# A hybrid mLSTM and S5 decoder step: TensorE's order in the S5 part written by hand, S5 tables on all 128 partitions

## The chip, the cores and the metric

The kernel runs on one core of one Trainium2 chip. The metric is device time in microseconds (us) of one execution, as the median of several runs. The engines are named as the profile names them: PE is TensorE (PEld its weight loads), DVE is VectorE, ACT is ScalarE, POOL is GpSimd, and SP is SyncE, whose queue issues nearly all DMAs.

## What is computed

One layer of a decoder trunk, for a prompt of 1,024 tokens and a sample batch of 8 sequences with 4 tokens each, in fp32. Cut to what matters here:

```python
a = rmsnorm(h, ln_mix)                      # [1056 tokens, 1024]
proj = a @ w_in
x_m, z_m, o_m, i_pre, f_pre, x_s, z_s = jnp.split(proj, SPLIT_IDX, axis=-1)   # 512 columns each, gates 4 + 4

# S5: 32 groups of 16 channels, each with 64 complex states
a_re, a_im = mag * cos(li * dt), mag * sin(li * dt)
bu = einsum('blgc,gpc->blgp', u, g * B)                 # complex
xs = associative_scan(x_t = a * x_{t-1} + bu_t)         # complex, along the tokens
y  = Re(einsum('blgp,gcp->blgc', xs, C)) + d_skip * u
yB = gelu(y);  yB = yB * sigmoid(yB @ w_glu + b_glu) * silu(z_s)

hA = mlstm_chunkwise(conv, gates, x_m, z_m, o_m)        # four heads
h  = h + concat([hA, yB]) @ w_out
h  = h + sigmoid(h @ w_ple_gate) * rmsnorm(p @ w_ple)
y  = rmsnorm(h, ln_final)
```

The final states of the mLSTM, the convolution and the S5 part are outputs too.

## The kernel before

**Products.** Large products are made in fp32 precision from two parts of each operand. `wtile` (L94) loads a weight tile, ACT casts it to its leading part `hi` (L111), and GpSimd subtracts that from the weight, which leaves the remainder `lo` (L112). `mm3` (L115 to L118) then runs three matmuls: hi by hi, hi by lo, lo by hi. `mtile` makes one 128-column block of the projection for all tokens, in three token pieces of 256, 384 and 416 columns (`CH`), with 8 steps of the contraction each: 3 x 8 x 3 = 72 products. The blocks are called xs0 to xs3 (x_s), xm0 to xm3, zm0 to zm3 and zs0 to zs3; `o_tile` and `o_rest` make the output gate o_m, token-major, and the mLSTM gates.

**The S5 part.** A group's channels are taken eight tokens at a time. `s5_x` writes a block of x_s to DRAM (`d_us`). The set-up (L313 to L493) makes, for all groups, powers of a (`pwr`, `pwi`), the rotation factors (`rAr` to `rBi`), the input matrices (`Bbr`, `Bbi`, stacked real over imaginary part as `Bs`), the output matrices `Cr`, `Ci`, and the initial states `x0s`. Its vectors lie on 128 partitions as (two groups, 64 states).

Then eight turns follow, u = 0 to 7, with four groups each. `s5_mats(u)` (L495) makes the tables: `wtr`, `wti` (products of powers and B: six DVE operations, `cmul` on V), their transposes `tpW` on PE, copied to `WV` by ACT; `cs` (products of powers and C: four GpSimd operations of 128 x 288 and four DVE operations of 64 x 288, one for each half of the partitions); the Toeplitz kernels `kp` on PE, copied to `ks`, stored to `dK` in DRAM and read back as the Toeplitz matrix `tz`; and the rotation tables `rtr`, `rti` (six GpSimd operations of 128 x 256). `s5_run(u)` (L564) then makes `vr` and `vi` on PE from `us` and `WV`, rotates them into `w` (DVE), runs four scans into `zr` and `zi` (DVE), rotates back into `v` (three operations on DVE, `v[2]` on GpSimd), adds them up as `xs_` (four DVE operations of 64 x 256, real over imaginary part by group), and multiplies by `tz` and `cs` on PE into `py`, on which ACT and DVE make the GELU (`sq`, `y2`, `ysm`). Eight stores `d_y` send y2 to DRAM.

**What sets the order.** Pools and tiles only order what depends on each other; the order on each engine comes from a scheduler, which takes the program's order with priorities. `tc.high_priority()` puts the S5 turns and the evacuations ahead of the rest, and the scheduler fills PE's gaps with what comes later in the program:

```python
    for j in range(1, 4):
        xsw.append(xs_w(j))
        for c in range(3):
            s5_x(j, c)
    with tc.high_priority():
        for u in range(8):
            mats = s5_mats(u)
            s5_run(u, mats)
    s5_final()
```

So xs1 to xs3 run while DVE makes the set-up, and xm0, `o_rest`, xm1 and zm0 fill PE's gaps in the S5 turns. After the S5 part come the first sample heads, zm, zs, and head 0 of the mLSTM, whose first state products are called `nu` (L984).

Of the kernel before, what the change touches and what calls it, by code (L numbers as in the profile page):

```python
# [23 lines left out]
CH = ((0, 256), (256, 384), (640, 416))  # L24
LOC = tuple((c, 128 * (i - b)) for i, (c, b) in enumerate(((0, 0),) * 2 + ((1, 2),) * 3 + ((2, 5),) * 4))
# [3 lines left out]
def tile_hymba(ctx: ExitStack, tc: tile.TileContext, d: dict, o: list):  # L29
# [27 lines left out]
    # ------------------------------------------------------------------ phase 1  # L57
# [67 lines left out]
    # ---------------- normalised input, transposed, in two parts  # L125
# [18 lines left out]
    def x_tile(i, xt):  # L144
# [8 lines left out]
        else:  # L153
            # the first tile in halves
# [19 lines left out]
    def mtile(hi, lo, evac, name, cs=(0, 1, 2)):  # L174
        for c in cs:
            t0, n = CH[c]
            ps = pm([128, 416], f"ps_{name}")
            for k in range(8):
                mm3(ps[:, :n], hi[:, k, :], lo[:, k, :], aTh[c][:, k, :n], aTl[c][:, k, :n], k == 0, k == 7)
            with tc.high_priority():  # L180
                evac(c, t0, n, ps)

    # ------------------------------------------------------------------ gates and output gate (token major)
# [15 lines left out]
    def o_tile(hh, ws, i):  # L199
        n = NH[hh]  # L200
# [3 lines left out]
        for k in range(8):  # L204
            hi, lo = ws[k // 4]
            mm3(ps[:m, :n], aTh[c][:, k, off:off + m], aTl[c][:, k, off:off + m],
                hi[:, k % 4, :], lo[:, k % 4, :], k == 0, k == 7)
        with tc.high_priority():
# [37 lines left out]
    def s5_x(j, c):  # L246
        if c == 0:
# [14 lines left out]
        mtile(*xsw[j], evac, "xs", (c,))  # L262
# [24 lines left out]
    # small parameters: rows -> columns by one transpose  # L287
# [26 lines left out]
    # ------------------------------------------------------------------ S5  # L314
# [44 lines left out]
    # bases e^{i theta 2^l}, l = 1..9, and rho = |a|^8  # L359
# [19 lines left out]
    # powers a^0 .. a^8 : [128, 16, 9]  # L379
# [17 lines left out]
    # rotation tables: fine A = E^1..E^8, coarse Bt = E^0, E^8, .., E^120 with E = e^{8 i theta}  # L397
# [16 lines left out]
    # input matrices times the ZOH factor  # L414
# [19 lines left out]
    Bbr = s5c.tile([128, 16, 16], F32, name="Bbr")  # L434
    Bbi = s5c.tile([128, 16, 16], F32, name="Bbi")
# [3 lines left out]
    # the same with real part over imaginary part, by group  # L439
# [3 lines left out]
    def stack(dst, re, im):  # L443
        # dst [128, .., 32 or fewer groups, ..]: from (g2 p) halves to (re/im p) halves
# [6 lines left out]
    # output matrices, transposed: [(g2 p), q, c']  # L451
    Cr = s5c.tile([128, 16, 16], F32, name="Cr")
    Ci = s5c.tile([128, 16, 16], F32, name="Ci")
# [8 lines left out]
    # initial states of the sequences: [(g2 p), b, q]  # L462
# [10 lines left out]
    # diagonal selector and D  # L473
# [21 lines left out]
    def s5_mats(u):  # L495
        q0 = 2 * u
        qs = slice(q0, q0 + 2)
        wtr = s5.tile([128, 2, 8, 16], F32, tag="wtr", name="wtr")
        wti = s5.tile([128, 2, 8, 16], F32, tag="wti", name="wti")
        u1 = s5.tile([128, 2, 9, 16], F32, tag="u1", name="u1", bufs=2)  # L500
        u2 = s5.tile([128, 2, 9, 16], F32, tag="u2", name="u2", bufs=2)

        def p4(ap, n):
            return ap.unsqueeze(3).to_broadcast([128, 2, n, 16])

        def b4(ap, n):
# [20 lines left out]
        u1 = s5.tile([128, 2, 9, 16], F32, tag="u1", name="u1", bufs=2)  # L527
# [121 lines left out]
    for j in range(1, 4):  # L649
        xsw.append(xs_w(j))  # L650
        for c in range(3):
            s5_x(j, c)
# [815 lines left out]
```

## Time and profile before

| | |
|---|---|
| median of 3 runs | 683.53 us (682.38 to 684.18) |
| span of the profiled execution | 678.6 us |
| PE busy | 621.7 us, 92%, 4,068 instructions |
| DVE busy | 451.6 us, 67%, 1,257 instructions |
| ACT busy | 252.2 us, 37% |
| POOL busy | 256.4 us, 38%, 269 instructions |
| chain that ended last | PE 56%, DVE 26%, DMA 6%, issue 5%, ACT 3%, POOL 2% |

The span runs from the first to the last instruction; the metric holds a little more than that. Busy times are unions of an engine's instructions over the whole span, so they average over stages with different limits. A stage is read from the windows, which give the same figures for a stretch of time. In the rows of instructions the first number is the start, the second the duration in us, then come engine, line, operation, output <- inputs, shape and count, and in brackets how long the engine sat idle before it and what ended that wait.

### The profile page before, as it was taken

The page shows a single profiled execution, that of the slowest core. Times are in us where ns is not written, and L with a number is a line of the kernel's source. Part 1 is how long each engine was busy: PE and PEld are TensorE (multiplying, and loading weights), DVE is VectorE, ACT ScalarE, POOL GpSimd, SP SyncE. Part 2 cuts the span into 40 slices and gives each one's busy share as a digit, 9 for nine tenths or more (in the row PEclk, how much of TensorE's full clock was granted, in tenths as well). Part 3 has the DMA queues.
Part 4 walks back from the last instruction along what each step waited for, and adds up shares of the span by engine and source line. Part 5 has one row for each costly group of instructions (what it writes and reads, how often), then busy time and mean ns, then how long its engine had stood idle before and what let it go on. Part 6 is the DMA issues. An engine that isn't in the chain of part 4 may idle for free.

```text
span 678.6 us, 11611 instructions
## 1 busy us (share of the span) xinstructions
PE 621.7 (92%) x4068; PEld 543.6 (80%) x4068; DVE 451.6 (67%) x1257; ACT 252.2 (37%) x623; POOL 256.4 (38%) x269
## 2 busy tenths in 40 slices
PE   3998996987888897999999998999999999999995
PEld 2997995776767896899898978867888877788885
DVE  4779758999999966358678579966222324566435
ACT  5553331232232346314445253555111324443332
POOL 5712347665565126243533246583011203001000
PEclk9999998999979999999999998999999999999998
DMA  8804341153325366225345373577541246313111
GB/s 279 233 32 98 112 129 51 47 130 93 88 58 129 82 165 213 64 75 156 114 154 151 101 195 133 170 256 233 185 144 42 94 162 237 140 32 124 56 70 62
DMA packets 109679, 86.34 MB, mean 127 GB/s; under 512 B 33263, under 2 KB 92547, under 8 KB 109622
## 3 DMA queue, kind: packets, MB, share of 16 engines
q1 hardware_dynamic: 109622, 85.61, 41.9%
q8 instruction: 32, 0.52, 0.3%
q14 instruction: 25, 0.20, 0.1%
HBM read 60.10 MB, written 25.49 MB: 126 GB/s over the span
## 4 chain that ended last, share of the span: by engine, by line
PE 56%; DVE 26%; DMA 6%; issue 5%; ACT 3%; POOL 2%; SPq 1%; DVEq 0%; POOLq 0%; ACTq 0%
PE po L1287 5%; PE po L1289 4%; PE po L1288 4%; PE po L1396 4%; PE po L1398 4%; PE po L1397 4%; PE ps_zs L116 2%; PE ps_zs L117 2%; PE ps_zs L118 2%; DVE cs L533 2%; DVE cs L526 1%; SPq L35 1%; DVE zr L590 1%; DVE u L373 1%; PE pe L1377 1%
## 5 line engine op out<-in xcount | busy, mean ns | idle before, releaser
L1396 PE MATMUL po<-wgh,hTh 128*128 128x512 f32 (+1 forms) x136 | 52.1, 383 | 0.0
L1398 PE MATMUL po<-wgh,hTl 128*128 128x512 f32 (+1 forms) x136 | 51.5, 379 | 0.0
L1397 PE MATMUL po<-wgl,hTh 128*128 128x512 f32 (+1 forms) x136 | 51.4, 378 | 0.0
L116 PE MATMUL ps_o<-hi_o,aTh 128*128 128x264 f32 (+2 forms) x136 | 41.0, 302 | 0.7 <-ACT aTh L171 0.7
L117 PE MATMUL ps_o<-lo_o,aTh 128*128 128x264 f32 (+2 forms) x136 | 40.2, 296 | 1.4 <-POOL lo_o L112 1.4
L118 PE MATMUL ps_o<-hi_o,aTl 128*128 128x264 f32 (+2 forms) x136 | 40.4, 297 | 0.0
L116 PE MATMUL ps_xs<-aTh,hi_xs 128*128 128x256 f32 (+2 forms) x96 | 32.3, 337 | 2.5 <-DVE gates L218 2.5
L116 PE MATMUL ps_xm<-aTh,hi_xm 128*128 128x256 f32 (+2 forms) x96 | 33.8, 352 | 0.0
L116 PE MATMUL ps_zs<-aTh,hi_zs 128*128 128x256 f32 (+2 forms) x96 | 32.2, 335 | 0.7 <-DVE ztmp L666 0.7
L1287 PE MATMUL po<-woh,mh 128*128 128x512 f32 x80 | 32.6, 408 | 0.0
L117 PE MATMUL ps_xm<-aTl,hi_xm 128*128 128x256 f32 (+2 forms) x96 | 32.4, 338 | 0.0
L118 PE MATMUL ps_xs<-aTh,lo_xs 128*128 128x256 f32 (+2 forms) x96 | 32.1, 334 | 0.0
L118 PE MATMUL ps_zm<-aTh,lo_zm 128*128 128x256 f32 (+2 forms) x96 | 32.0, 334 | 0.0
L118 PE MATMUL ps_xm<-aTh,lo_xm 128*128 128x256 f32 (+2 forms) x96 | 32.0, 333 | 0.0
L117 PE MATMUL ps_xs<-aTl,hi_xs 128*128 128x256 f32 (+2 forms) x96 | 31.8, 332 | 0.0
L1288 PE MATMUL po<-wol,mh 128*128 128x512 f32 x80 | 31.8, 397 | 0.0
L118 PE MATMUL ps_zs<-aTh,lo_zs 128*128 128x256 f32 (+2 forms) x96 | 31.8, 331 | 0.0
L1289 PE MATMUL po<-woh,mlo 128*128 128x512 f32 x80 | 31.8, 397 | 0.0
L116 PE MATMUL ps_zm<-aTh,hi_zm 128*128 128x256 f32 (+2 forms) x96 | 31.7, 331 | 0.0
L117 PE MATMUL ps_zm<-aTl,hi_zm 128*128 128x256 f32 (+2 forms) x96 | 31.7, 330 | 0.0
L117 PE MATMUL ps_zs<-aTl,hi_zs 128*128 128x256 f32 (+2 forms) x96 | 31.5, 328 | 0.0
L1296 DVE TENSOR_TENSOR hTl<-tr,hTh 128x512 fp32r<-128x512 f32 x16 | 11.0, 690 | 30.3 <-ACT hTh L1295 30.1
(587 smaller groups left out, 2043.4 us busy)
## 6 DMA issues: line engine op xcount, KB each, us to landing
xt<-in_x_prompt SPq DMA_DIRECT2D x15, 512.0 KB
Wraw<-in_w_out SPq DMA_DIRECT2D x16, 256.0 KB
Wraw<-in_w_ple_gate SPq DMA_DIRECT2D x16, 256.0 KB
d_h<-xt SPq DMA_DIRECT2D x8, 512.0 KB
h_t<-d_h SPq DMA_DIRECT2D x8, 512.0 KB
out<-g_t SPq DMA_DIRECT2D x14, 256.0 KB
mt<-d_m SPq DMA_DIRECT2D x10, 256.0 KB
d_us<-xs SPq DMA_DIRECT2D x32, 72.0 KB
```

What stands on the lines that cost most here:

```text
L35: nc.sync.dma_start(out, in_)
L116: T.matmul(ps, wh, xh, start=first, stop=False)
L117: T.matmul(ps, wh, xl, start=False, stop=False)
L118: T.matmul(ps, wl, xh, start=False, stop=last)
L533: V.scalar_tensor_tensor(cs[64:128, g2:4:2], u1[ph], -1.0, u2[ph], op0=MUL, op1=SUB)
L1287: T.matmul(ps, mh[:, k % 4, :], hi, start=k == 4, stop=False)
L1288: T.matmul(ps, mh[:, k % 4, :], lo, start=False, stop=False)
L1289: T.matmul(ps, mlo[:, k % 4, :], hi, start=False, stop=k == 3)
L1296: V.tensor_tensor(hTl[i][:, 4 * q:4 * q + 4, :], tp, hi.bitcast(F32), op=SUB)
L1396: T.matmul(ps[:, :b - a], hTh[i][:, k, :], hi[:, ws], start=k == 4, stop=False)
L1397: T.matmul(ps[:, :b - a], hTh[i][:, k, :], lo[:, ws], start=False, stop=False)
L1398: T.matmul(ps[:, :b - a], hTl[i][:, k, :], hi[:, ws], start=False, stop=k == 3)
```

## The change

1. **PE's order is written in the kernel** from xs1 to the end of the S5 part. `mtile`, `o_tile`, `o_rest`, `s5_x` and `z_tile` become generators that yield after three products with the columns they took; `s5_mats` and `s5_run` yield between their steps. Inside `tc.manual_schedule` for PE the loop below takes S5 steps (`prod`) and, between them, a given number of columns of filler (`take`). Filler is xs1, xs2, xs3, `o_rest`, zs0 and zs1, in this order. The other engines stay with the scheduler.
2. **The tables wt and cs are built stacked**, real over imaginary part on 128 partitions, by two products and a sum on DVE each: `wt` 128 x 512, `cs` 128 x 576. New stacked operands `Bj`, `pdr`, `pdi`, `Cs`, `Cj` come from 20 ACT copies in the set-up. GpSimd makes no part of cs any more.
3. `v[2]` moves from GpSimd to DVE. `tz`, `y2`, `WV`, `u1`, `u2` have one buffer instead of two; the rotation tables stay on GpSimd, with one scratch tile `u3`. `Bbr`, `Bbi`, `Cr`, `Ci` move to the set-up's pool, and a new pool holds the stacked operands.
4. `o_rest()`, `zs_tile(0)` and `zs_tile(1)` are taken out of their later place. Comments are dropped.

```diff
+FILL_A, FILL_B, FILL_C = 14500, 600, 1200
...
-    def mtile(hi, lo, evac, name, cs=(0, 1, 2)):
+    def mtile_g(hi, lo, evac, name, cs=(0, 1, 2)):
...
                 mm3(ps[:, :n], hi[:, k, :], lo[:, k, :], aTh[c][:, k, :n], aTl[c][:, k, :n], k == 0, k == 7)
+                if k < 7:
+                    yield 3 * n
...
+    stack(lambda ph, g2: pdr[ph, g2:32:2, :], pwr, pwr)
+    stack(lambda ph, g2: pdi[ph, g2:32:2, :], pwi, pwi)
...
+        A.copy(Cs[0:64, g2:32:2, :], Cr[ph])
+        A.mul(Cs[64:128, g2:32:2, :], Ci[ph], -1.0)
+        A.mul(Cj[0:64, g2:32:2, :], Ci[ph], -1.0)
+        A.mul(Cj[64:128, g2:32:2, :], Cr[ph], -1.0)
...
-        cmul(V, wtr, wti, a_r, a_i, b4(Bbr[:, qs], 8), b4(Bbi[:, qs], 8), u1[:, :, :8], u2[:, :, :8])
+        def table(dst, b1, b2, n):
+            u1 = s5.tile([128, 4, 9, 16], F32, tag="u1", name="u1", bufs=1)
+            u2 = s5.tile([128, 4, 9, 16], F32, tag="u2", name="u2", bufs=1)
+            V.tensor_tensor(u1[:, :, :n], p4(pdr, n), b4(b1, n), op=MUL)
+            V.tensor_tensor(u2[:, :, :n], p4(pdi, n), b4(b2, n), op=MUL)
+            V.tensor_tensor(dst, u1[:, :, :n], u2[:, :, :n], op=ADD)
+        wt = s5.tile([128, 4, 8, 16], F32, tag="wt", name="wt")
+        table(wt, Bs, Bj, 8)
+        yield
...
-        G.tensor_tensor(u1, a_r, c_r, op=MUL)
-        G.tensor_tensor(u2, a_i, c_i, op=MUL)
-        for g2 in range(2):
-            ph = slice(64 * g2, 64 * g2 + 64)
-            V.tensor_tensor(cs[0:64, g2:4:2], u1[ph], u2[ph], op=SUB)
...
+        table(cs, Cs, Cj, 9)
+        yield WV
...
-        tz = s5.tile([128, 4, 128], F32, tag="tz", name="tz", bufs=2)
+        tz = s5.tile([128, 4, 128], F32, tag="tz", name="tz", bufs=1)
...
-        G.tensor_tensor(v[2], zr, Ri, op=MUL)
+        V.tensor_tensor(v[2], zr, Ri, op=MUL)
...
+    with tc.manual_schedule(engines={mybir.EngineType.PE}):
+        mats = [s5_mats(u) for u in range(8)]
+        prod(mats[0])
+        WV = prod(mats[0])
+        take(3000)
+        for u in range(8):
+            run = s5_run(u, WV, lambda: parts)
+            prod(run)
+            parts = prod(mats[u])
+            prod(run)
+            if u < 7:
+                prod(mats[u + 1])
+            take(FILL_A)
+            prod(run)
+            take(FILL_B)
+            if u < 7:
+                WV = prod(mats[u + 1])
+                take(FILL_C)
+            prod(run)
+        s5_final()
+        for _ in fill:
+            pass
```

How this moves instructions, at three places. The lines of after lie a few to 80 lines further down. First PE in before, where the products of xs0 have just ended; `ps_xs` here is xs1, `tp` names are transposes:

```order
L460 MATMUL tpC<-ident,cn 128x128
L710 MATMUL tpr<-ident,gin 32x128
L116 MATMUL ps_xs<-aTh_104,hi_xs_1049 128x256
L117 MATMUL ps_xs<-aTl_107,hi_xs_1049 128x256
L118 MATMUL ps_xs<-aTh_104,lo_xs_1050 128x256
L116 MATMUL ps_xs<-aTh_104,hi_xs_1049 128x256
L117 MATMUL ps_xs<-aTl_107,hi_xs_1049 128x256
L118 MATMUL ps_xs<-aTh_104,lo_xs_1050 128x256
```

The same place on PE in after:

```order
L492 MATMUL tpC<-ident,cn 128x128
L790 MATMUL tpr<-ident,gin 32x128
L492 MATMUL tpC<-ident,cn 128x128 x3
L790 MATMUL tpr<-ident,gin 32x128
L510 MATMUL tpX<-ident,sn__1033 128x128
L825 MATMUL tpk<-ident,g__2833 128x32
L510 MATMUL tpX<-ident,sn__1038 128x128
L559 MATMUL tpW<-ident,wt 128x128 x4
L117 MATMUL ps_xs<-aTh_104,hi_xs_1098 128x256
L118 MATMUL ps_xs<-aTl_107,hi_xs_1098 128x256
```

The set-up's transposes (C, gates, initial states) and the first tpW now stand ahead of xs1, whose 216 products with those of xs2 and xs3 are spread over the first turns.

Second, DVE from the end of one turn to the first w of the next, in before (`u` are table scratch tiles):

```order
L602 TENSOR_TENSOR xs__1676<-v_1679,v_1680 64x2x128 x2
L603 TENSOR_TENSOR xs__1676<-v_1681,v_1682 64x2x128 x2
L374 TENSOR_TENSOR wtr<-u_1852,u_1853 128x256
L542 SCALAR_TENSOR_TENSOR ks<-dsel,Dt,ks 128x16
L578 TENSOR_TENSOR w_1786<-vr,rtr 128x256
L579 TENSOR_TENSOR w_1787<-vi,rti 128x256
L580 TENSOR_TENSOR w_1788<-vi,rtr 128x256
L581 TENSOR_TENSOR w_1789<-vr,rti 128x256
L375 TENSOR_TENSOR u_1852<-pwr,Bbi 128x2x128
L376 TENSOR_TENSOR u_1853<-pwi,Bbr 128x2x128
L584 TENSOR_TENSOR w_1786<-w_1786,w_1787 128x256
L585 TENSOR_TENSOR w_1788<-w_1788,w_1789 128x256
```

The same stretch in after, from xs_ of one turn to the first w of the next:

```order
L636 TENSOR_TENSOR xs__1717<-v_1720,v_1721 64x2x128 x2
L637 TENSOR_TENSOR xs__1717<-v_1722,v_1723 64x2x128 x2
L653 SCALAR_TENSOR_TENSOR sq<-sq,py 128x272 x2
L655 SCALAR_TENSOR_TENSOR y_1668<-sq,py 128x256
L657 SCALAR_TENSOR_TENSOR ysm<-sq,py 128x16
L552 TENSOR_TENSOR wt<-u_1902,u_1903 128x512
L655 SCALAR_TENSOR_TENSOR y_1668<-sq,py 128x256
L550 TENSOR_TENSOR u_2049<-pdr,Cs 128x576
L551 TENSOR_TENSOR u_2050<-pdi,Cj 128x576
L657 SCALAR_TENSOR_TENSOR ysm<-sq,py 128x16
L612 TENSOR_TENSOR w_1867<-vr,rtr 128x256
```

In before the next turn's w follow xs_ and the GELU of the turn (`sq`, `y`, `ysm`) comes later, among them; in after sq, y and ysm follow xs_ directly, wt's sum and two products of cs stand between them, and the next w come behind.

Third, GpSimd over about one turn of the S5 part, in before:

```order
L598 TENSOR_TENSOR v_1553<-zr,rti 128x256
L593 MEMSET xs__1676 128x4
L372 TENSOR_TENSOR u_1637<-rBr,rAr 128x256
L373 TENSOR_TENSOR u_1638<-rBi,rAi 128x256
L374 TENSOR_TENSOR rtr<-u_1637,u_1638 128x256
L375 TENSOR_TENSOR u_1637<-rBr,rAi 128x256
L376 TENSOR_TENSOR u_1638<-rBi,rAr 128x256
L377 TENSOR_TENSOR rti<-u_1637,u_1638 128x256
L522 TENSOR_TENSOR u_1740<-pwr,Cr 128x288
L523 TENSOR_TENSOR u_1741<-pwi,Ci 128x288
L593 MEMSET xs__1804 128x4
L529 TENSOR_TENSOR u_1746<-pwr,Ci 128x288
```

And in after, where one turn is seven rows:

```order
L591 TENSOR_TENSOR u_2107<-rBi,rAi 128x256
L590 TENSOR_TENSOR rti<-rBr,rAi 128x256
L590 TENSOR_TENSOR rtr<-rBr,rAr 128x256
L592 TENSOR_TENSOR rtr<-rtr,u_2107 128x256
L591 TENSOR_TENSOR u_2107<-rBi,rAr 128x256
L592 TENSOR_TENSOR rti<-rti,u_2107 128x256
L627 MEMSET xs__2132 128x4
L591 TENSOR_TENSOR u_2300<-rBi,rAi 128x256
L590 TENSOR_TENSOR rti<-rBr,rAi 128x256
```

The rows L522 to L530 (cs) and L598 (v) are gone, and the six rows of the rotation tables and a memset stay.

## Rows read from the trace of the kernel before

**Rows 1.** Windows: stretch, length, busy PE, PEld, DVE, ACT, POOL, clock, DMA, GB/s.

```profile
64.00:104.00 40.00, 37.54 (x239) 36.38 (x239) 28.79 (x129) 13.47 (x40) 17.52 (x16) 0.96 0.41 118
104.00:233.00 129.00, 105.26 (x824) 90.69 (x819) 125.42 (x287) 34.68 (x115) 76.30 (x89) 0.95 0.35 86
233.00:250.00 17.00, 17.00 (x103) 16.86 (x104) 10.34 (x30) 9.30 (x17) 2.40 (x1) 1.00 0.51 128
196.00:204.00 8.00, 7.57 (x37) 5.09 (x37) 7.97 (x8) 0.64 (x2) 8.00 (x7) 0.57 0.06 19
```

**Rows 2.** The source view of L578, the first w of a turn.

```profile
L578 DVE TENSOR_TENSOR w<-vr,rtr x8: 405/418/427, 108.3 to 220.6; 128x256 f32<-128x256 f32 x8
```

**Rows 3.** PE: the last py of the S5 part, and the first nu.

```profile
232.29 0.40 PE L610 MATMUL py<-xs__2316,cs 128*128 128x136 f32 x2
...
286.64 0.38 PE L984 MATMUL nu<-v,nmb 128*128 128x129 f32 x2
```

**Rows 4.** DVE and SP between the set-up and the first turn.

```profile
83.21 0.41 DVE L711 COPY rw<-tpr 32x256 f32<-32x256 f32 x1 [3.31 <-PE tpr L710]
...
86.03 1.18 SPq L35 DMA_DIRECT2D d_us<-xs  x2
...
87.31 0.72 SPq L35 DMA_DIRECT2D er<-ends  x1
...
89.75 0.15 DVE L726 TENSOR_TENSOR_SCAN mc<-er 4x8 f32<-4x8 f32 x1
...
92.82 0.27 DVE L731 TENSOR_SCALAR M__2437<-M__2437,mp 32x128 f32<-32x128 f32 x1 [2.26 <-DMA mp<-mc]
```

**Rows 5.** Prices on DVE, GpSimd and ACT, alone and beside each other; last the page.

```profile
63.27 2.31 DVE L372 TENSOR_TENSOR cu<-rAr,bas_r 128x16 f32<-128x16 f32 x1
...
65.49 0.17 DVE L373 TENSOR_TENSOR cu<-rAi,bas_i 128x16 f32<-128x16 f32 x1
...
165.25 0.84 DVE L597 TENSOR_TENSOR v<-zi,rti 128x256 f32<-128x256 f32 x1
...
170.37 1.24 DVE L603 TENSOR_TENSOR xs__1804<-v,v 64x256 f32<-64x256 f32 x2
...
170.02 0.86 POOL L523 TENSOR_TENSOR u<-pwi,Ci 128x288 f32<-128x288 f32 x1
...
171.64 0.42 DVE L372 TENSOR_TENSOR u<-pwr,Bbr 128x256 f32<-128x256 f32 x1
171.98 0.42 DVE L373 TENSOR_TENSOR u<-pwi,Bbi 128x256 f32<-128x256 f32 x1
...
187.03 0.87 DVE L603 TENSOR_TENSOR xs__1932<-v,v 64x256 f32<-64x256 f32 x2
...
189.68 0.40 ACT L613 ACTIVATE sq<-py 128x272 f32<-128x272 f32 x1
...
L1296 DVE TENSOR_TENSOR hTl<-tr,hTh 128x512 fp32r<-128x512 f32 x16 | 11.0, 690 | 30.3 <-ACT hTh L1295 30.1
```

**Rows 6.** PE inside a turn, and after the S5 part.

```profile
182.79 0.64 PE L538 MATMUL kp<-cs,Bs 128*32 128x128 f32 x8
...
184.49 0.39 PE L117 MATMUL ps_o<-lo_o,aTh 128*128 128x256 f32 x1
...
189.00 0.38 PE L514 MATMUL tpW<-ident,wtr 128*128 128x128 f32 x2
...
250.39 1.95 PE L941 MATMUL vps<-wv,xm 128*128 128x128 f32 x16
...
259.78 1.13 PE L959 MATMUL qps<-xc,Gm 128*128 128x512 f32 x2 [3.44 <-DVE xc L925]
```

**Rows 7.** SP's queue in a turn.

```profile
138.70 3.81 SPq L35 DMA_DIRECT2D d_y<-y  x8
...
142.61 0.54 SPq L35 DMA_DIRECT2D dK<-ks  x1
...
145.12 0.62 SPq L35 DMA_DIRECT2D tz<-dK  x1
```

More of the change, by code (lines that the diff above doesn't have):

```diff
@@ L199, in o_tile, with o_tile_g @@
     def o_tile(hh, ws, i):
+        for _ in o_tile_g(hh, ws, i):
+            pass
+    def o_tile_g(hh, ws, i):
         n = NH[hh]
@@ L246, in s5_x, with s5_x_g @@
     def s5_x(j, c):
+        for _ in s5_x_g(j, c):
+            pass
+    def s5_x_g(j, c):
         if c == 0:
@@ L312, in tile_hymba @@
     xphase.close()
+    s5d = s5x.enter_context(tc.tile_pool(name="s5d", bufs=1, side="right", reuse_waits="tile"))
     s5t = ExitStack()
@@ L450, in tile_hymba @@
     stack(lambda ph, g2: Bs[ph, g2:32:2, :], Bbr, Bbi)
-    Cr = s5c.tile([128, 16, 16], F32, name="Cr")
-    Ci = s5c.tile([128, 16, 16], F32, name="Ci")
+    Bj = s5d.tile([128, 32, 16], F32, name="Bj")
+    pdr = s5d.tile([128, 32, 9], F32, name="pdr")
+    pdi = s5d.tile([128, 32, 9], F32, name="pdi")
+    for g2 in range(2):
+        ph = slice(64 * g2, 64 * g2 + 64)
+        A.mul(Bj[0:64, g2:32:2, :], Bbi[ph], -1.0)
+        A.copy(Bj[64:128, g2:32:2, :], Bbr[ph])
+    stack(lambda ph, g2: pdr[ph, g2:32:2, :], pwr, pwr)
+    stack(lambda ph, g2: pdi[ph, g2:32:2, :], pwi, pwi)
+    Cr = s5p.tile([128, 16, 16], F32, name="Cr")
+    Ci = s5p.tile([128, 16, 16], F32, name="Ci")
     for t_, s_ in ((Cr, "s5_C_re"), (Ci, "s5_C_im")):
@@ L461, in tile_hymba @@
             A.copy(t_[:, 8 * half:8 * half + 8, :], tp.rearrange("p (q c) -> p q c", c=16))
+    Cs = s5d.tile([128, 32, 16], F32, name="Cs")
+    Cj = s5d.tile([128, 32, 16], F32, name="Cj")
+    for g2 in range(2):
+        ph = slice(64 * g2, 64 * g2 + 64)
+        A.copy(Cs[0:64, g2:32:2, :], Cr[ph])
+        A.mul(Cs[64:128, g2:32:2, :], Ci[ph], -1.0)
+        A.mul(Cj[0:64, g2:32:2, :], Ci[ph], -1.0)
+        A.mul(Cj[64:128, g2:32:2, :], Cr[ph], -1.0)
     x0r = s5c.tile([128, 8, 16], F32, name="x0r")
@@ L528, in s5_mats, with p4, b4 @@
[L528 to L533 removed]
+        gs = slice(4 * u, 4 * u + 4)
+        def p4(t_, n):
+            return t_[:, gs, 0:n].unsqueeze(3).to_broadcast([128, 4, n, 16])
+        def b4(t_, n):
+            return t_[:, gs].unsqueeze(2).to_broadcast([128, 4, n, 16])
@@ L535, in s5_mats @@
+        yield
+        tp = pt([128, 4, 128], "tpW")
+        for g in range(4):
+            T.transpose(tp[:, g, :], wt[:, g].rearrange("p s c -> p (s c)"), ident)
+        WV = s5.tile([128, 4, 128], F32, tag="WV", name="WV", bufs=1)
+        A.copy(WV, tp)
+        cs = s5.tile([128, 4, 9, 16], F32, tag="cs", name="cs", bufs=2)
+        table(cs, Cs, Cj, 9)
+        yield WV
         kp = pt([128, 128], "kp")
@@ L611, in s5_run @@
                          start=False, stop=True)
+        yield
+        for q, ps in enumerate(pys):
             sq = s5.tile([128, 2, 136], F32, tag="sq", name="sq", bufs=2)
@@ L647, in s5_final, with z_tile_g @@
         dma(o_pim[0, 0], ob[:, 64:128])
[L649 to L652, printed above, removed]
-    with tc.high_priority():
-        for u in range(8):
-            mats = s5_mats(u)
-            s5_run(u, mats)
-    s5_final()
-    s5x.close()
     def z_tile(c0, idx, name):
+        for _ in z_tile_g(c0, idx, name):
+            pass
+    def z_tile_g(c0, idx, name):
         hi, lo = wtile(wcols(c0, 128), 8, 128, name)
@@ L667, in evac, with filler, take, prod @@
             dma(d_z[idx, :, t0:t0 + n], tz_[:, :n])
-        mtile(hi, lo, evac, name)
+        yield from mtile_g(hi, lo, evac, name)
+    def filler():
+        for j in range(1, 4):
+            xsw.append(xs_w(j))
+            for c in range(3):
+                yield from s5_x_g(j, c)
+        yield from o_rest()
+        for j in range(2):
+            yield from z_tile_g(2056 + 128 * j, 4 + j, f"zs{j}")
+    fill = filler()
+    def take(cols):
+        for n in fill:
+            cols -= n
+            if cols <= 0:
+                break
+    def prod(gen):
+        with tc.high_priority():
+            return next(gen)
+    with tc.manual_schedule(engines={mybir.EngineType.PE}):
[19 more added lines that the diff above has]
+        for _ in fill:
+            pass
+    s5x.close()
     SC = 128.0 ** -0.5
```

66 lines of the change are left out of this document (26 added, 40 removed).

## The prediction

> **What bounds the kernel now.** I read the page's busy times first: PE is busy for 621.7 of the 678.6 us span, so a gain is PE waiting less, or PE doing its work sooner somewhere. The windows say where it waits [rows 1]. From 104 to 233 us, the S5 part, PE is busy 105.26 of 129 us while DVE is busy 125.42; from 233 to 250 PE has no gap at all. So DVE paces the S5 part, and PE is held up there by a chain of eight turns: w, scans, v, xs_ on DVE, py on PE, Square on ACT, sq and y on DVE. The source view of the first w shows the pace: eight of them from 108.3 to 220.6, so seven periods of 16.05 us [rows 2]. The last py starts at 232.29, and the first nu of head 0, at 286.64, is the place from which both orders of PE are word for word the same to the end [rows 3]. **Everything that the change does must show by how much earlier that nu starts**; what follows it is PE-bound and keeps its length.
>
> The profiled execution's span is 678.6; the median of the runs is 683.53, so 4.9 us lie outside the span. I carry the 4.9 over.
>
> **Part 1: the front.** The 216 products of xs1 to xs3 no longer stand between the table set-up and S5. PE thus has next to nothing to do from 64 us until wt(0) is there. What ends last there? Before, DVE waited 3.31 us at rw for a transpose (tpr) that stood behind those products on PE [rows 4]; after, PE is free and this wait goes. SP issued er behind two d_us stores of xs1 (1.18 us) [rows 4], which are later now. So er goes out at 87.31 - 3.31 - 1.18 = 82.8. The two round trips through DRAM that the gate sequence makes on DVE's own queue stay: er to mc 2.44, mc to M 3.07 [rows 4], so M comes at 88.3. Behind M now stand one 576-column sum, four small operations and the three wt(1) operations, some 3.0 us: **first w at 91.3, against 108.3**, 17 us sooner. The new stacked operands cost 20 ACT copies of about .4 us. The eight of pdr/pdi and those of Cr stand early in ACT's order, beside DVE's set-up; only Bj and the last of Cs and Cj follow Bbi and Ci, and they are done before mc comes: no cost. If that cover were gone, each would cost its .4 us.
>
> **Part 2: the period, uncontended.** A 256-element DVE operation takes a step of .34 (171.64 to 171.98), a pair of xs_ .87, a 512-element one .69 at most [rows 5]. One turn of after: six w and four v at .34 = 3.4, four scans at .34 = 1.3, four xs_ 1.7, sq, y, ysm and ks 1.6, three wt at .62 = 1.9, three cs at .68 = 2.0: 12.0 us. Against before, ten table operations of 256 and 288 elements a partition become six of 512 and 576, on twice the partitions for cs, and v[2] adds .34: on DVE's own time the two versions are nearly equal. In DVE's new order nothing stands between xs_ and sq, so it waits there for half the py and a Square: xs_ ended at 187.90 and all py were through at 189.00, half of that is .6, Square takes .40 [rows 5, 6], with hand-overs 1.3. Before, the next w stood in that gap. Sum 13.3.
>
> **Part 3: contention with GpSimd.** Per turn, GpSimd loses four 288-element table operations and v[2], and keeps the six of the rotation tables. A pair of xs_ takes .87 alone and 1.24 while GpSimd works on a table operation of .86 [rows 5]: .19 per DVE operation; a v takes .84 instead of .34 [rows 5]: .50. The six rotation operations start when v has released the table, so they fall on the four xs_ (.75), on the py gap and on sq and y, which read PSUM. I take 1.0, with ends of 0 (all in the gap) and 3.0 (six times .50). The split of a weight (lo) holds a 16-element DVE operation for 2.31 where .17 is usual [rows 5]; three of them fall into the seven periods: up to 2.1 each, I take 6 us in all, .9 per period. Together 15.2. The first two turns also hold the gate's small operations, 1 us in all: **seven periods take 107.4, against 112.35.**
>
> The row of xs_ shows a share of a GpSimd operation handed on, not the whole of it; the row of the 2.31 shows the whole. The Trainium skill, "SBUF — State Buffer", section "Who interferes with whom", says that a DVE instruction with two SBUF inputs and a GpSimd instruction that reads SBUF exclude each other, the loser blocking fully. The row of lo agrees, that of xs_ only in part. By the rule each collision would cost nearly a whole GpSimd operation; what that would make of the time is the third rival below.
>
> **Part 4: PE in a turn.** The 24 S5 products before a turn's fill take 184.49 - 182.79 = 1.7, py 1.1, tpW and small ones .7: 3.5 [rows 6]. Fill is 14,500 + 600 + 1,200 columns. 103 products took 17.00 [rows 1], .165 each; a tile's 72 products have 352 columns on average, so 16,300 columns are 46 products, 7.6 us. PE needs 11.1 of 15.2: it doesn't bound the loop, and about 4 us per turn are waits. wt is made two turns ahead and cs one, so tpW and kp don't wait for tables. v[2] and y2, WV, tz with one buffer: y2's stores are issued before the next y; WV is free once vr and vi are through; no cost found. tz is a rival below.
>
> **Part 5: from the last py to nu.** w(7) starts at 91.3 + 107.4 = 198.7; w to the end of py is 9.2 of DVE plus 1.3: 209.2. Before, 232.7 to 286.64 is 53.9 us for 252 products (41.6), a wait of 3.44 at qps for xc [rows 6], some 1 us of other waits, so 7.9 of small products. After, the filler is shorter there and 390 products stand in this place (zs0's rest, zs1, xm0, xm1, zm0, zm1): 390 x .165 = 64.4, the 7.9, and head 1's vps, 1.95 [rows 6]: 74.3. xc is ready long before qps now: no wait. **nu at 283.5 instead of 286.6: 3.1 us gained.** Span 675.5, time 680.4.
>
> The sum shows how thin this is: loop and front end 23.5 us sooner, and 138 products more behind them give 20.4 back. In other words PE's idle time shrinks by only 3 us: a hole of some 20 us opens at the front, and less waiting in the loop pays for it. Each us of mean period is 7 us of time; 15.6 is break-even.
>
> **The rivals.**
> *Faster, rotation tables in the gap.* All six fall on py's gap and on the PSUM readers, and one lo instead of three meets a two-input operation: period 14.0, 8.4 us less: 672. For it: sq and y stand right behind, 2 us of PSUM readers. Against it: GpSimd starts just when xs_ does.
> *No gain, the pace stays.* DVE was already 97% busy and its own work is unchanged; if collisions merely move from tables to other operations, the period stays 16.05: 680.4 + 5.0 (seven periods of 112.35 instead of 107.4) = 685.4; with part of the gain, 683. This is also the case in which the change doesn't do what it says.
> *Slower, the full lock.* If every rotation operation stops a two-input operation for .50, contention is 3.0 instead of 1.0: 14 us more, 694. It decides from 1.6 us of contention per turn on.
> *Slower, tz.* On SP dK waits behind the eight d_y stores (3.81), then tz is issued 2.51 after dK [rows 7]. In after, y ends just ahead of the next w, so dK goes out about 3.9 and tz 6.4 us after w, and py wants it 9.2 after. tz has one buffer, so nothing is ahead. If it lands 4.4 after its issue rather than 2.8 or less, each py waits 1.6: 11 us, 692.
> *Slower, the clock.* At 196 to 204 the granted clock was .57 on average, the lower of the two levels (1.2 of 2.4 GHz) for most of it, while PE had waited shortly before [rows 1]. After, PE waits in each turn. If most turns run at the lower level, PE needs some 15 of its 15.2 us, and py and vr, on DVE's chain, cost about .7 more per turn: 5.6 us, 686. The Trainium skill, "TensorE: Matmul & The Clock Gate", section "HAM oscillation — how this bites in real kernels", also has gaps between bursts bring the lower level; the row agrees.
>
> **How the numbers follow.** Forecast .36 (676 to 685 by its own bounds, contention .4 to 1.6); gap .17 (672); pace stays .14 (683 to 686); full lock .09 (694); tz .10 (692); clock .14 (686). A measurement of this kernel can tell some 0.3%, 2 us, from no change. Faster by that (below 681.5): .60 of the forecast, all of the gap, a few of the others: .43. Within: .25 of the forecast, half of the unchanged pace, a third of the clock, and some of tz: .24. Slower: the rest, .33. The likeliest case gives 680.4; the range from 670 to 692 leaves the best half of the gap and the full lock out.
>
> **What would show it.** Right: first w near 91; the eight first w 15.2 apart; xs_ pairs near 1.2; a PE wait of some 1.5 us before most py, put down to xs_ and not to tz; an S5 part that ends near 209; PE without gaps from there to nu at 283.5. Wrong: w's period at 14 or above 15.8; PE waiting for vr because WV or wt is late; a granted clock near .5 through the loop; a first w after 95, when the two round trips on SP or ACT's copies come later than I have them; or waits after 209 for weights of zs1 and xm.

## The result: 702.85 us, 3% slower

The changed kernel takes 702.85 us (median of 4 runs, 702.55 to 706.65) against 682.95 us for the kernel before (median of 4): a ratio of 1.0307, 95% interval 1.0275 to 1.0340. The forecast was 680.4 with a range from 670 to 692. The profiled execution's span is 700.8 us.

The windows of after over the stretches of [rows 1], in the same columns:

```profile
64.00:104.00 40.00, 19.60 (x104) 16.12 (x105) 38.70 (x134) 16.51 (x50) 23.80 (x22) 0.65 0.27 75
104.00:233.00 129.00, 103.45 (x804) 95.02 (x802) 98.04 (x244) 37.17 (x118) 37.03 (x41) 0.90 0.36 91
233.00:250.00 17.00, 17.00 (x94) 16.85 (x94) 3.98 (x12) 4.25 (x10) 3.69 (x2) 0.90 0.61 161
```

In [rows 1] PE had 37.54 us of work in the first stretch, now 19.60; 105.26 in the second, now 103.45. So by 233 us PE has been busy for 19.8 us less (37.54 + 105.26 against 19.60 + 103.45), close to the 20 us that the result is longer; what PE has not done by then it does behind the S5 part. GpSimd's busy time in the S5 part is halved (76.30 to 37.03), and DVE's falls from 125.42 to 98.04: DVE no longer paces the turns, it waits. The pace is read from the source view of the first w, as in [rows 2] (min, median and longest ns, then first and last start):

```profile
L612 DVE TENSOR_TENSOR w<-vr,rtr x8: 409/415/424, 90.0 to 215.9; 128x256 f32<-128x256 f32 x8
```

From 90.0 to 215.9: the first w is 18 us sooner than before, and the seven periods last 18.0 us each on average instead of 16.05. They are not alike: 20.3, 20.7, 16.7, 16.6, 16.4, 18.5 and 16.8. The view of PE's waits in the S5 part (what waits, for what: us in all, times, longest) shows a new first row:

```profile
PE py L646 <- DMA tz<-dK: 19.6, 7, 4.5
PE py L646 <- DVE sfr L675: 2.7, 1, 2.7
...
PE tpg L683 <- ACT ob L680: 1.6, 1, 1.6
```

The only row of before for tz in its S5 part:

```profile
PE py L609 <- DMA tz<-dK: 1.6, 1, 1.6
```

That wait is behind this read of tz, by SP's queue and PE's timeline in before:

```profile
210.98 0.62 SPq L35 DMA_DIRECT2D tz<-dK  x1
```

```profile
216.72 0.47 PE L609 MATMUL py<-us,tz 128*128 128x136 f32 x2 [1.56 <-DMA tz<-dK]
```

One turn of after, put together from the timelines of three engines (start, length, engine, line, operation, and in brackets what it waited for), shows the whole loop. DVE, from the first w to ks:

```profile
199.14 0.41 DVE L612 TENSOR_TENSOR w<-vr,rtr 128x256 f32<-128x256 f32 x1
...
201.13 0.23 DVE L573 SCALAR_TENSOR_TENSOR ks<-dsel,Dt,ks 128x16 f32<-128x16 f32 x1
```

SP's queue, the y stores, dK and tz:

```profile
199.16 3.14 SPq L36 DMA_DIRECT2D d_y<-y  x5
202.41 0.53 SPq L36 DMA_DIRECT2D dK<-ks  x1
...
204.86 0.63 SPq L36 DMA_DIRECT2D tz<-dK  x1
```

PE, py with its wait for tz:

```profile
209.30 0.79 PE L646 MATMUL py<-us,tz 128*128 128x136 f32 x2 [3.77 <-DMA tz<-dK]
209.88 0.66 PE L647 MATMUL py<-xs__2325,cs 128*128 128x136 f32 x2
210.34 0.66 PE L646 MATMUL py<-us,tz 128*128 128x136 f32 x2
```

DVE, sq behind Square, and the next turn's first w:

```profile
211.92 0.44 DVE L653 SCALAR_TENSOR_TENSOR sq<-sq,py 128x272 f32<-128x272 f32 x1 [5.62 <-ACT sq L652]
...
215.94 0.42 DVE L612 TENSOR_TENSOR w<-vr,rtr 128x256 f32<-128x256 f32 x1
```

ks is written by 201.36, 2.2 us after the turn's first w. dK goes out at 202.41, behind five d_y stores; tz is issued 2.45 later, when dK has landed; py starts 4.44 after that, having waited 3.77. From py to the next w are 6.64: Square waits for half of the py, which at this moment take .45 to .46 a step where the rows of before have .23, DVE sat idle for 5.62 before sq, and the next vr comes by way of tpW and WV only when py is through. 2.2 + 1.05 + 2.45 + 4.44 + 6.64 = 16.8, from one w to the next with no gap. This is the last of the seven periods, in which DVE has the sum of the last cs and no other table to make. **The trip of tz through DRAM closes a loop: kp, ks, dK, tz, py, tpW, WV, vr, and the next kp.** In all eight turns tz is issued 2.4 to 2.5 us after dK, and py follows that issue after 3.9 to 4.8 us in the seven turns that wait for it.

From the last py to nu the forecast nearly held: 76.7 us from the end of py, at 229.93, to the first nu at 306.59 (286.64 in [rows 3]), where 74.3 were forecast. In PE's timeline of after the last py is the row

```profile
229.53 0.40 PE L647 MATMUL py<-xs__2516,cs 128*128 128x136 f32 x2
```

and the first nu is the row

```profile
306.59 0.39 PE L1064 MATMUL nu<-v,nmb 128*128 128x129 f32 x2
```

### The profile page after: what moved, and what is told of

It is laid out like the page before. It is cut to its first block, busy times and chain, and to the rows that moved or that the text cites. A ratio compares the mean times of both kernels' runs of the same rounds, so it can differ in the third digit from the quotient of the medians.

```text
span 700.8 us, 11530 instructions
## 1 busy us (share of the span) xinstructions
PE 627.8 (90%) x4068; PEld 553.0 (79%) x4068; DVE 431.9 (62%) x1233; ACT 262.2 (37%) x643; POOL 226.6 (32%) x229
## 4 chain that ended last, share of the span: by engine, by line
PE 64%; DVE 15%; DMA 11%; ACT 4%; issue 3%; SPq 2%; POOL 0%; POOLq 0%; DVEq 0%; ACTq 0%
PE po L1364 4%; PE po L1366 4%; PE po L1365 4%; PE po L1473 4%; PE po L1474 3%; PE po L1475 3%; DMA tz<-dK 3%; SPq L36 2%; PE ps_xm L117 2%; PE ps_xm L119 2%; PE ps_xm L118 2%; PE py L646 2%; PE ps_zs L117 2%; PE ps_zs L119 2%; DMA dK<-ks 2%
## 5 line engine op out<-in xcount | busy, mean ns | idle before, releaser
L646 PE MATMUL py<-us,tz 128*128 128x136 f32 x64 | 19.3, 398 | 22.3 <-DMA tz<-dK 19.6
L117 PE MATMUL ps_xs<-aTh,hi_xs 128*128 128x256 f32 (+2 forms) x96 | 34.0, 355 | 0.0
L646 PEld LDWEIGHTS py<-us,tz 128*128 128x128 f32 x64 | 15.1, 286 | 24.0 <-DMA tz<-dK 5.8
```

The lines of the kernel that those rows point to most:

```text
L117: T.matmul(ps, wh, xh, start=first, stop=False)
L646: T.matmul(ps[:, g2, :], tz[:, g, :], us[:, g, 0:136], start=True, stop=False)
```

## The experiments

Every kernel was timed against the kernel before on its chip; ratios are to that. The kernel before took 682.95 to 685.80 us in these comparisons, so differences in us between rows of different chips are good to some 3 us, and the ratios are the better measure. First w, last py and first nu are start times in each kernel's trace, and the period is the mean of its seven; what the trace holds behind the first nu is its span less the first nu.

| run | median us | ratio (95%) | first w | mean period | last py | first nu |
|---|---|---|---|---|---|---|
| before | 682.95 | 1 | 108.3 | 16.05 | 232.3 | 286.6 |
| after | 702.85 | 1.0307 (1.0275 to 1.0340) | 90.0 | 18.00 | 229.5 | 306.6 |
| e1 kp ahead | 693.93 | 1.0138 (1.0095 to 1.0181) | 95.0 | 16.69 | 221.3 | 297.1 |
| e2 more filler | 692.90 | 1.0115 (1.0068 to 1.0162) | 90.2 | 19.03 | 234.6 | 289.6 |
| e3 tables only | 676.41 | 0.9882 (0.9844 to 0.9919) | 105.1 | 14.37 | 216.7 | 277.3 |
| e4 order only | 715.83 | 1.0452 (1.0414 to 1.0490) | 91.6 | 19.59 | 242.1 | 319.3 |
| e5 front filled | 686.25 | 1.0016 (0.9990 to 1.0043) | 97.0 | 18.46 | 236.1 | 291.5 |
| e6 kp ahead, front filled | 684.62 | 1.0018 (0.9991 to 1.0046) | 98.5 | 17.89 | 233.8 | 287.8 |
| e7 tables, two tz | 676.74 | 0.9890 (0.9851 to 0.9929) | 105.5 | 14.61 | 218.8 | 277.8 |
| e8 e6 with zm and more filler | 688.16 | 1.0063 (1.0039 to 1.0088) | 97.0 | 17.16 | 229.6 | 286.1 |
| e9 e6 with vr ahead of py | 673.13 | 0.9853 (0.9814 to 0.9891) | 97.4 | 15.78 | 220.3 | 277.4 |
| e10 e9 with more filler | 689.00 | 1.0086 (1.0056 to 1.0116) | 97.8 | 18.15 | 236.1 | 275.7 |
| e11 e9 without the front | 698.49 | 1.0197 (1.0142 to 1.0251) | 91.4 | 17.46 | 227.3 | 304.8 |
| e12 d_y on ACT's queue | 704.16 | 1.0306 (1.0266 to 1.0345) | 90.9 | 17.06 | 224.8 | 306.4 |

**Which half of the change costs (e3, e4).** e3 takes the new tables and leaves PE's order to the scheduler; e4 takes the hand-written order with the tables of before.

```diff
 e3:
-    with tc.manual_schedule(engines={mybir.EngineType.PE}):
-        mats = [s5_mats(u) for u in range(8)]
...
+    for j in range(1, 4):
+        xsw.append(xs_w(j))
+        for c in range(3):
+            s5_x(j, c)
+    with tc.high_priority():
+        for u in range(8):
...
+    for _ in o_rest():
+        pass
...
+    zs_tile(0)
+    zs_tile(1)
 e4:
-            V.tensor_tensor(u1[:, :, :n], p4(pdr, n), b4(b1, n), op=MUL)
...
+        cmul(V, wtr, wti, a_r, a_i, b4(Bbr[:, qs], 8), b4(Bbi[:, qs], 8), u1[:, :, :8], u2[:, :, :8])
...
-        V.tensor_tensor(v[2], zr, Ri, op=MUL)
+        G.tensor_tensor(v[2], zr, Ri, op=MUL)
```

Expected of e3: 

> The tables of the change (wt and cs stacked, v[2] on DVE, one buffer for tz, y2 and WV) without the hand-written order: PE's order is left to the scheduler, xs1 to xs3, o_rest and zs stand where they stood before. If tables without GpSimd save contention as forecast (1 us or more per turn): 673 to 679. If they save nothing: 681 to 685. If one buffer for tz costs by itself: py waits for tz, and the time is above 686.

Expected of e4: 

> The hand-written order of the change with the tables of before (wtr, wti on DVE, cs and v[2] on GpSimd), one buffer for tz, y2 and WV as in the change. Theory A: the loop over tz sets the period here too, 18 to 18.6, and DVE's extra contention lies in its free time: 702 to 708. If the new tables were what costs: 685 or less.

The tables alone are a gain of 1.2%, and the order alone a loss of 4.5%; .9882 x 1.0452 is 1.0329, the ratio of the change within its interval. So the two ratios multiply to that of the change, and the order is what costs. In e3 the source view of the first w reads

```profile
L612 DVE TENSOR_TENSOR w<-vr,rtr x8: 385/418/425, 105.1 to 205.6; 128x256 f32<-128x256 f32 x8
```

100.5 us for seven periods, 14.37 each: 1.7 us less per turn than before. In e4 py waits for tz in seven turns, as in after, for 24.4 us, so the loop over tz comes with the order with either set of tables.

**The loop over tz (e1).** cs and kp, and with them ks, dK and tz, a turn ahead of their use.

```diff
-        tz = s5.tile([128, 4, 128], F32, tag="tz", name="tz", bufs=1)
+        tz = s5.tile([128, 4, 128], F32, tag="tz", name="tz", bufs=2)
-        xs_ = s5.tile([128, 4, 137], F32, tag="xs_", name="xs_", bufs=2)
+        xs_ = s5.tile([128, 4, 137], F32, tag="xs_", name="xs_", bufs=1)
...
-            take(FILL_A)
+            take(7000)
+            if u < 7:
+                parts = prod(mats[u + 1])
+            take(FILL_A - 7000)
```

Expected: 

> The changed kernel with one thing moved: cs and kp of a turn, and with them ks, dK and the read of tz, come a turn earlier in PE's order (after 7,000 columns of the turn before's filler), with two buffers for tz and, to make room, one for xs_. Theory A, the round trip of tz closes the loop (kp, ks, dK, tz, py, WV, the next vr, the next kp): no py waits for tz, the period of w falls from 18.0 to 15 to 16, seven periods give back 14 to 20 us, time 683 to 689. Theory B, the lower clock of PE in the turns makes the chain long and the wait for tz only stands in front of it: the period stays above 17 and the time above 695.

No py waits for tz any more, and the time falls by 9 us, to 693.93 (by the ratios 1.7%, 11.5 us): between the two expectations. The period is 16.69. One reason is the edit itself: in this order kp(0) stands ahead of tpW(0), which delays the first w by 5 us. The other is in the waits: DVE still stands 13.4 us in twelve waits for Square (25.6 in sixteen in after). Taking tz out shows the next chain behind it, not a free turn.

**Filling the wait (e2).** `FILL_A = 21500` instead of 14500.

Expected: 

> The changed kernel with FILL_A 21,500 instead of 14,500 columns, nothing else. Theory A: 7,000 columns are 3.3 us of products, put into a wait for tz of 2 to 4.5 us; the period stays near 18 (at most 18.5), PE's waits at py fall from 19.6 us to under 6, and some 18 us less work is left after the S5 part: time 684 to 689. Theory B, or one by which PE's products bound the turns: the period grows by up to 3.3 us to 21 and the time stays within 3 us of 703.

py's waits for tz fall from 19.6 to 1.5 us, as theory A has it, but the period grows by 1.0 us, above the 18.5 that it allows. The first nu starts 17.0 us sooner than in after (289.6 against 306.6), nearly the 18 expected; from nu to the end of the trace, however, e2 takes 401.9 us and after 394.2. So 10 us of gain are left. What makes the stretch behind nu longer is open.

**The hole at the front (e5).**

```diff
         prod(mats[0])
+        take(40000)
         WV = prod(mats[0])
```

Expected: 

> The changed kernel with the first 40,000 columns of filler (xs1 and half of xs2, some 19 us of products) put ahead of the first tpW, where PE was busy for only 9.5 of the 26 us from 64 to 90; nothing else. Theory C, the hole at the front costs its own length, since that work then stands behind the S5 part: 15 to 19 us less, 684 to 688, with the turns as long as in the change (18 us). Theory D, the hole is free, because only the chain of the turns counts: 699 to 703.

686.25, 16.6 us less than the change (by the ratios 2.9%, 19.9 us), with turns no shorter than there (18.46; this trace is of the slowest of its ten runs, 691.55): the hole costs about its length. The windows of the same 26 us show it, with PE busy for 20.17 instead of 9.49 us and the granted clock at 1.00 instead of .54. After:

```profile
64.00:90.00 26.00, 9.49 (x49) 6.81 (x50) 25.11 (x105) 14.73 (x44) 15.76 (x13) 0.54 0.36 103
```

e5:

```profile
64.00:90.00 26.00, 20.17 (x127) 19.27 (x127) 21.75 (x103) 16.90 (x47) 13.02 (x13) 1.00 0.43 121
```

**Both together (e6), and with more filler (e8).** e6 has e5's line and e1's edit, with kp(0) left behind vr(0) and the other kp after 11,000 columns; e8 also appends zm0 and zm1 to the filler and sets FILL_A to 17,500.

Expected of e6: 

> Both together: kp, ks, dK and tz of turns 1 to 7 a turn ahead (after 11,000 columns of filler, so that kp doesn't wait for cs; turn 0 as in the change, so that the first w isn't later), and 40,000 columns ahead of the first tpW. If tz's loop (theory A) and the hole (theory C) are separate causes that add up: 702.9 - 17 for the hole - 14 for seven periods of 16 instead of 18, 670 to 676. If they share what they give back: 684 or more. If it beats the tables alone (676.4), the hand-written order is worth something once its two losses are gone.

Expected of e8: 

> As the run with both together, with zm0 and zm1 appended to the filler and FILL_A 17,500 instead of 14,500 (1.4 us more of products per turn), since PE still waits 1 to 4 us for xs_ before each py. If those waits can be filled: 7 to 11 us below the run with both together, some 663 to 667. If PE then bounds the turns: the same time as that run, or more.

Both came out at their second alternative. e6 is at 684.62, no better than e5 by the ratios, although only one py waits for tz (3.0 us). The two do not add up: in e6 something else takes the place of the wait for tz. DVE's waits in e6 (us in all, times, longest), of which the first row is the point:

```profile
DVE sq L658 <- ACT sq L657: 13.6, 14, 1.9
DVE xs L270 <- DMA d_us<-xs: 4.2, 1, 4.2
```

14 waits for Square, 13.6 us. The order of after puts the next tpW, and so vr and w, behind py: DVE has little to do from its last xs_ until py and Square are through. That is not all: in e6's fifth period, 21.5 us, two splits of a weight on GpSimd hold up DVE's scans by some 4 us (rows in the last section), and no run takes that apart. e8's turns are shorter than e6's (17.16 a period) and its nu 1.7 us sooner, but from nu to the end it takes 399.8 us where e6 takes 393.9. So its loss lies behind nu, and it does not show whether more products in the turns help.

**vr ahead of py (e9).** e6, and the next turn's tpW, vr and vi ahead of this turn's py. The columns of filler in a turn stay the same, but stand elsewhere, and kp comes after 5,000 of them instead of 11,000:

```diff
-            prod(run)
-            take(FILL_B)
-            if u < 7:
-                WV = prod(mats[u + 1])
-                take(FILL_C)
+            if u < 7:
+                WV = prod(mats[u + 1])
+                take(2500)
+                nxt = s5_run(u + 1, WV, lambda v=u + 1: parts[v])
+                prod(nxt)
+            take(4000)
+            prod(run)
+            take(FILL_B + FILL_C)
```

Expected: 

> The run with kp ahead and the front filled, and in addition tpW, vr and vi of the next turn ahead of py of this one in PE's order, so that DVE has the next w to do while PE makes py and ACT squares it. Theory E, what the hand-written order still costs is that vr of a turn stands behind py of the turn before (py, tpW, WV, vr in one chain, while DVE waits 2 to 3 us per turn for Square): the period falls from 16 to 18 to about 14.5 as under the scheduler, 15 to 20 us less than 684.6, 665 to 671; at least 676. Theory F, the weight splits on GpSimd (lo) and the gate's small operations set the long turns whatever PE's order: 680 to 685.

673.13, 11.5 us below e6 and below both kernels of this case (ratio .9853 to before; the tables alone are at .9882, and the two intervals overlap). Theory E had 665 to 671, or 676 at the least gain, with a period of 14.5: the sign and the mechanism are right, the size is somewhat large. DVE's waits for Square are gone, as its view of waits in e9 shows:

```profile
DVE w L617 <- issue: 4.0, 1, 4.0
...
DVE sq L658 <- ACT sq L657: 0.8, 2, 0.5
```

The first w's source view in e9:

```profile
L617 DVE TENSOR_TENSOR w<-vr,rtr x8: 388/412/424, 97.4 to 207.8; 128x256 f32<-128x256 f32 x8
```

Square costs .8 us instead of 13.6, and no PE wait for tz is left; the period is 15.78. DVE is busy for 104.75 of the 110.4 us of these seven periods, so it paces the turns again, as it did before.

**Around e9 (e10, e11).** e10 has 18,500 columns of filler per turn instead of 14,500; e11 is e9 without the 40,000 columns ahead of the first tpW.

Expected of e10: 

> The same with 18,500 instead of 14,500 columns of filler in a turn (1.9 us more of products). If PE has free time in the turns at the period of theory E (14.5 against some 11 us of products): 5 to 10 us less than the run before it, 658 to 666. If PE's products then bound the turns: the same within 3 us.

Expected of e11: 

> The order with vr and kp of the next turn ahead of py, without the 40,000 columns ahead of the first tpW: the front of the change, the turns of the fast version (673.1). If hole and turns add up: 673.1 + 17 = 690, and 13 below the change. If the hole is free once the turns are short: 673 to 676. If the turns need the front's lead: above 695.

e10 missed both of its ranges with 689.00. Its first three periods are 16.0, 15.4 and 14.2, then four of 18.6 to 22.0 follow. In the two longest PE is busy for 18.75 of 22.0 and 19.49 of 21.8 us, at a granted clock of .84 and .92: there are 69 and 83 large products in them, where the 18,500 columns with FILL_B's and FILL_C's 1,800 are 58 by the 352 columns of a product. So these turns are nearly filled with products. But that is not where e10 loses its time, since fewer products are left behind the turns. The first nu, in e10 and then in e9:

```profile
275.71 0.38 PE L1079 MATMUL nu<-v,nmb 128*128 128x129 f32 x2
```

```profile
277.39 0.38 PE L1079 MATMUL nu<-v,nmb 128*128 128x129 f32 x2
```

e10 is 1.7 us ahead there, and then takes 413.1 us to the end of the trace where e9 takes 395.5. So the 16 us are lost behind nu; by what, the runs don't settle. That the rest keeps its length from nu on held for the change itself (394.2 against 392.0), and not for e2, e8 and e10.

e11 takes 698.49, its third alternative: without the front's lead its second turn lasts 27.2 us, in which DVE sits idle for 5.5 us until a read of the gates' values from DRAM (senm) and for 3.0 us until vr. So the hole and the turns are not two separate terms either.

**SP's queue (e7, e12).** e7 is e3 with two buffers for tz; e12 is the change with the d_y stores on ACT's queue (`nc.scalar.dma_start` in place of `dma`).

Expected of e7: 

> The tables alone under the scheduler's order, with two buffers for tz instead of one (and one for xs_, to make room). If the one buffer costs in the scheduler's order, where py waited 10 us in four waits for tz and for ks: 668 to 673. If not: 675 to 678.

Expected of e12: 

> The changed kernel with the eight d_y stores of a turn issued from ACT's queue instead of SP's, nothing else. There dK goes out 1.0 to 1.4 us after ks, behind d_y; if this stands on the chain of the turns (ks, dK, tz, py), each period falls by some 1 us: 693 to 697. If another chain of the same length stands beside it (py, Square, w), or ACT's issuing takes back what SP gains: 701 to 705.

e7 is at 676.74: one buffer for tz costs nothing in the scheduler's order. In e12 dK follows ks closely and the period falls by .94 us, from 18.00 to 17.06, as priced. But the time does not fall. In the last turn tz goes out later behind dK than in the others. SP's queue in e12, the last two turns:

```profile
197.26 0.53 SPq L36 DMA_DIRECT2D dK<-ks  x1
...
199.85 0.61 SPq L36 DMA_DIRECT2D tz<-dK  x1
...
212.31 0.53 SPq L36 DMA_DIRECT2D dK<-ks  x1
...
217.03 0.63 SPq L36 DMA_DIRECT2D tz<-dK  x1
```

PE's waits in e12, the first two rows:

```profile
PE py L646 <- DMA tz<-dK: 20.8, 7, 4.2
PE tpg L683 <- ACT ob L680: 5.4, 1, 5.4
```

tz is issued 4.72 after dK there, not 2.5; why is open. The wait at tpg is the edit's own doing, by ACT's timeline in e12 behind the last turn:

```profile
227.38 4.52 ACTq L659 DMA_DIRECT2D d_y<-y  x8
232.00 0.27 ACT L680 COPY ob<-tpf 128x128 f32<-128x128 f32 x1 [5.11 <-DMA d_y<-y]
```

The eight stores now stand on ACT's queue ahead of the copy `ob` for which PE's tpg waits. So the last py is 4.7 us sooner than in after, this wait, 3.8 us longer than there, takes most of it back, and the first nu, at 306.44, is where it was. This is the second alternative, ACT's issuing takes back what SP gains. A queue with neither the chain of the turns nor such a copy on it was not tried.

## Why the prediction was wrong

**The sum, term by term.** The forecast span is 675.5, the measured one 700.8. Of the 25.3 us between them, rounded, the front gives -1.3, the seven periods 18.6, the last turn from its w to the end of py 3.5, the stretch from there to nu 2.4, and what follows nu 2.2. A term that cancels part of it: the prediction put 4.9 us outside the span, but the runs of after have 1.75 there (702.55 and 700.8 in the profiled one). By that, the trace of before is of an execution some 3 us faster than the median, and this went into the 4.9.

**The front** came out close: first w forecast at 91.3, measured 90.0. DVE's wait for tpr is gone, as forecast. Two errors partly cancel in the rest: M came at 85.5 instead of 88.3, and what stood behind it on DVE took 4.5 us instead of 3.0.

**The period** failed: 15.2 forecast, 18.0 measured. Seven periods took 126.0 instead of 107.4 us. Its parts one by one:

- *DVE's own work* was right. In the periods from 147.67 and 164.31, which have the tables in them, DVE is busy for 13.1 and 13.0 us. Of that some 1.0 is contention on xs_, which leaves the 12 us of the sum.
- *Contention* was right too as far as the rotation tables go. The two pairs of xs_ in these turns take 1.18 and 1.60 beside GpSimd, and 1.7 together without it: some 1.0, as taken.
- *The loop over tz* is the step that failed. The sum let py start 9.2 us after w, so it left tz 2.8 us from its issue, and no row was looked up for that trip. "No cost found", it says of tz's one buffer, and the rest stood among the rivals, at .10. tz in fact was followed by py after 3.9 to 4.8 us in each turn that waited for it, and PE waited 19.6 us for it in all. The two rows of before shown with the result have a trip of 5.7 us. The prediction left them out, and looked at the number of tz's buffers and at SP's order instead of at where kp stands in PE's order. Before, kp of a turn stood ahead of the py of the turn before it [rows 6]; in the hand-written order it stands behind vr, and so behind the last py. That was to be seen in the change's code.
- *The rival's own price* was 692, 11 short. Its chain was right: tz followed by py after 4.4 us and 16.8 from w to w, which is what the turn shown above took, and four of the seven periods are 16.4 to 16.8. It missed the others: the first two, with the gate's small operations, took 20.3 and 20.7 where its price has 17.3, and one took 18.5. In the last turn w to the end of py took 14.0 instead of 12.1.
- *"PE needs 11.1 of 15.2: it doesn't bound the loop, and about 4 us per turn are waits"* is the second step that failed. PE had the time, but its order is fixed: the filler stands ahead of py, then PE waits, and what could run meanwhile (the next tpW and vr) stands behind. The sum had 1.3 for DVE's wait for Square and the hand-overs; DVE stood 25.6 us in sixteen such waits, 3.2 a turn. e9 shows what the place of vr costs with tz out of the way: 11.5 us.

**The rival of the clock** (.14, 686) was real as a mechanism and not the cause. The granted clock is .90 in the turns, and py's steps are doubled after a wait. In e2 the waits are filled and the clock is .96 from 90 to 235 us, and the period is longer, not shorter; in e9, with the chain itself changed, it is .96 too and the period is 15.78. So the clock rises when the waits are filled, and the pace does not follow it in e2. What it adds to a turn is py's doubled step, some 1 us by the 1.1 us that py had in the sum (an estimate).

**The full lock** (.09, 694) did not come about: it needs 3.0 us of contention from the rotation operations per turn, and the xs_ show 1.0.

**From the end of the last py to nu** it took 76.7 us, forecast 74.3; the waits at tpf and tpg (2.0 us) were missing in the sum. **The tail** after nu is 394.2 long, before 392.0: it nearly kept its length, as assumed. **The hole at the front** was seen, and its price of some 20 us too: e5 measures 16.6, or 19.9 by the ratios. The turns could pay for it only if they came out at 15.6 or less. The forecast said so, and then trusted a sum in which one link of the loop had no row.

## What to carry to other kernels

Before judging a hand-written order by busy times, follow one turn round: from an operation to the same operation of the next turn, through every engine and every DMA round trip, and give each link a row; a link without a row is the one to look up first. In an in-order queue, put the next turn's head (here tpW, vr, kp) ahead of this turn's tail (py), so that what an engine could do next does not stand behind another's round trip. Try the parts of a change apart: here one half gained 1.2% and the other lost 4.5%. And read where in the span a time is lost before explaining it: e10's turns are 2.4 us longer than e9's, but its loss lies behind them.

## What the hardware showed that I had not expected

A table store to DRAM and its read back take long. In after it is 2.4 to 2.5 us from the issue of dK to that of tz (4.72 in the last turn of e12), and 3.9 to 4.8 us from the issue of tz (128 x 512) to the py that waited for it, 6.9 us in all in the turn shown.

GpSimd's split of a weight stops DVE's scans for nearly all of its length. A pair of scans takes .73 alone in after (at 201.95), and in e6 two pairs took 2.88 and 2.81 beside two lo of 2.84 and 2.46. DVE's timeline in e6:

```profile
173.30 2.88 DVE L629 TENSOR_TENSOR_SCAN zr<-rho,w 128x128 f32<-128x128 f32 x2
176.11 2.81 DVE L629 TENSOR_TENSOR_SCAN zi<-rho,w 128x128 f32<-128x128 f32 x2
```

GpSimd's (POOL) over the same time:

```profile
173.06 2.84 POOL L113 TENSOR_TENSOR lo_zs<-raw_zs,hi_zs 128x1024 fp32r<-128x1024 f32 x1 [7.12 <-ACT hi_zs L112]
175.87 2.46 POOL L113 TENSOR_TENSOR lo_xm<-raw_xm,hi_xm 128x1024 fp32r<-128x1024 f32 x1
```

A rotation operation, in contrast, holds up an xs_ by less than its own length: a pair of xs_ in after took .84 with GpSimd idle and 1.60 beside rotation operations of some .8. DVE's timeline in after:

```profile
189.19 1.60 DVE L637 TENSOR_TENSOR xs__2132<-v,v 64x256 f32<-64x256 f32 x2
...
204.55 0.84 DVE L636 TENSOR_TENSOR xs__2325<-v,v 64x256 f32<-64x256 f32 x2
```

GpSimd's in after:

```profile
188.84 0.81 POOL L590 TENSOR_TENSOR rtr<-rBr,rAr 128x256 f32<-128x256 f32 x1
189.72 0.78 POOL L592 TENSOR_TENSOR rtr<-rtr,u 128x256 f32<-128x256 f32 x1
```

This bears on the Trainium skill, "SBUF — State Buffer", section "Who interferes with whom", by which a DVE operation with two SBUF inputs contends with a GpSimd operation that reads SBUF, for a port pair that is an exclusive lock. The lo agree, the rotation operations only in part (.38 per xs_).
